# A 512-byte write per DMA engine ahead of the first store, and the last tile stored in two pieces instead of four

## The chip, the cores and the metric

One core of a Trainium2 chip. The metric is the device time in microseconds (us) of one execution; lower is better.

## The reference

The input `x` is 32 x 512 x 2048 numbers of float32. With `x1` the first 1024 columns and `x2` the last 1024:

```python
silu_x1 = x1 * (1 / (1 + np.exp(-x1)))
return (silu_x1 * x2).astype(np.float32)
```

134.22 MB are read and 67.11 MB written, each byte once. There is no matrix product.

## The kernel before

The 16,384 rows are cut into 16 tiles (0 to 15) of 1024 rows: 128 partitions with K = 8 consecutive rows each, so that one partition's share is contiguous in memory, 64 KB of input and 32 KB of output. Loads are issued by ScalarE and stores by SyncE, so they stand on two DMA rings. A ring is a queue of transfers; each DMA here is cut into packets that 16 DMA engines carry (a load is 128 packets of 64 KB in the records), and at its end every engine writes 4 bytes: 560 such records for the 35 DMAs of the kernel before. I read them as the report of completion, since the trace has 560 landings as well, each 0.3 to 0.7 us after its record when both are paired in order of time. SBUF is the memory on the chip that holds the tiles, HBM the large memory that holds `x` and the output. Two input buffers and two output buffers hold whole tiles.

```python
K = 8
KC = 2
in_pool  = ctx.enter_context(tc.tile_pool(name="in_pool", bufs=2))
out_pool = ctx.enter_context(tc.tile_pool(name="out_pool", bufs=2))
# ... cut: plan, view(), the first load moved ahead of the start barrier
load(0)                       # nc.scalar.dma_start: the ring of the loads, q10 in the profile
load(1)
for i in range(n_tiles):
    xt = loaded.pop(i)
    last = i == n_tiles - 1
    ov = view(out_flat, i)
    ot = out_pool.tile([P, K, half], dt, name="ot")
    for c in range(0, k, KC):                 # four steps of 2 rows
        ce = min(c + KC, k)
        nc.scalar.activation(out=ot[:, c:ce, :], in_=xt[:, c:ce, :half], func=...Silu)
        nc.vector.tensor_mul(out=ot[:, c:ce, :], in0=ot[:, c:ce, :], in1=xt[:, c:ce, half:])
        if last:                              # the last tile leaves in four pieces
            nc.sync.dma_start(out=ov[:, c:ce, :], in_=ot[:, c:ce, :])
    if not last:                              # nc.sync: the ring of the stores, q1 in the profile
        nc.sync.dma_start(out=ov, in_=ot[:, :k, :])
    if i + 2 < n_tiles:
        load(i + 2)                           # this input buffer is free again
```

The load of tile i + 2 waits for the multiplies of tile i. Each store waits for multiplies.

## Time and profile before

| | before |
|---|---|
| median of the 3 runs | 470.78 us (470.76 to 470.87) |
| span of the profiled run | 468.87 us |
| DMA rate over the span | 429 GB/s |
| VectorE, ScalarE busy | 30%, 25% |

These lines are of the page of the kernel before: its span; the busy time of the engines; the mean busy share of the 16 DMA engines in 40 slices, in tenths; the packets; the two rings with packets, MB and the share of 16 engines' time; the chain of waits by engine and by line; and the DMA issues with their size in KB and the median time from issue to landing.

```profile
span 468.9 us, 269 instructions
...
DVE 142.3 (30%) x64; ACT 118.2 (25%) x65; POOL 0.2 (0%) x4
...
DMA  9899999999999998999999999999999989999998
...
DMA packets 5042, 201.35 MB, mean 429 GB/s; under 512 B 560, under 2 KB 560, under 8 KB 560
...
q10 hardware_dynamic: 2304, 134.22, 66.4%
q1 hardware_dynamic: 2736, 67.11, 33.2%
...
DMA 80%; DVE 15%; ACT 3%; DVEq 0%; issue 0%
DMA xt<-in_x_dram 80%; DVE ot L92 15%; ACT ot L87 3%; DVEq L128 0%
...
out_dram<-ot SPq DMA_DIRECT2D x15, 4096.0 KB, 39.8
out_dram<-ot SPq DMA_DIRECT2D x4, 1024.0 KB, 5.7
xt<-in_x_dram ACTq DMA_DIRECT2D x16, 47.1
```

The DMA row is at 9 nearly everywhere, and the two rings' packets take 66.4% + 33.2% = 99.6% of the engines' time. The chain of waits says the same from the other end: 80% of the span is waiting for loads. VectorE and ScalarE are idle for 70% and 75% of the span, and stand in the chain for 18% of it, mostly between a load's landing and the issue of the load two tiles later.

The end of the run, from the timeline of the kernel before (start, duration, engine, line, operation, how often, and the idle time before it with what ended it):

```profile
...
start us, us, engine line op out<-in xcount [idle before <-releaser]
451.03 7.31 ACT L87 ACTIVATE ot<-xt 128x2048 f32<-128x2048 f32 x4 [21.57 <-DMA xt<-in_x_dram]
452.97 8.90 DVE L92 TENSOR_TENSOR ot<-ot,xt 128x2048 f32<-128x2048 f32 x4 [19.98 <-ACT ot L87]
455.29 6.94 SPq L98 DMA_DIRECT2D out_dram<-ot  x4
```

The last tile's Silu begins when its load has landed, at 451.03 us; its first store piece is issued 4.26 us later, after the first multiply.

**The packet records.** The trace also has a record for each DMA packet: ring, start, duration and size, but not the engine. I strung them to engines by joining each record to one that ended within some 5 ns of its start. In the kernel before, an engine's string is gapless from its first packet to its last, but for a fetch of instructions (0.3 us) on two engines: a packet of 64 KB (load) takes 2.418 us, one of 32 KB (store) 1.213, one of 8 KB 0.309, and a completion write of 4 bytes 0.009. Here is one engine around the first store (start us, duration us, ring, bytes):

```
 33.264  2.441  q10 65536
 35.701  3.180  q10 65536     <- 0.76 us too long, once
 38.878  1.213  q1  32768     <- first packet of the first store
 40.087  2.418  q10 65536
 42.501  1.213  q1  32768
 43.711  0.009  q10 4         <- completion of a load: a turn of its own
 43.717  1.213  q1  32768
 44.926  2.418  q10 65536
```

From the first store on, the rings take strict turns, one packet each: of the 3,887 pairs of neighbours strung this way between 34 and 428 us, 3,869 change the ring. A 4-byte completion write uses a whole turn, like the one of 0.009 us at 43.711 us, which stands alone between two store packets. From start to start of its load packets (65,536 bytes in 2.414 us) this case makes 16 x 27.15 = 434.4 GB/s, and none of the 2,048 load packets took less than the usual 2.418 us. That no packet can be faster is my estimate from these numbers; it was not shown. If it holds, the only time to win lies where packets do not follow each other at that pace: 1.1 us before the first packet, about 0.6 us in the first load packets, 0.87 us per engine (mean of 16) in the long packet ahead of the first store, and 1.2 us from the last packet to the end of the span.

### The profile page before, as it was taken

The numbers are of one execution on the slowest core, as the hardware profiler recorded it, in microseconds if no ns is written. First come the engines' busy times: TensorE is split into PE (matmuls) and PEld (weight loads), VectorE is DVE, ScalarE is ACT, GpSimd is POOL, SyncE is SP. The second block draws the span as 40 slices with busy tenths as digits, with TensorE's granted clock in tenths as the row PEclk, the third lists the DMA queues.
The fourth block names the chain that finished last, engine by engine and source line by source line (L and its number), as shares of the span: only waits on it lengthen the run. The fifth ranks groups of instructions, "written<-read, shape, count | busy, mean of one in ns | idle before, by whom it ended". The sixth has DMA issues, their size and how long they took to land.

```text
span 468.9 us, 269 instructions
## 1 busy us (share of the span) xinstructions
DVE 142.3 (30%) x64; ACT 118.2 (25%) x65; POOL 0.2 (0%) x4
## 2 busy tenths in 40 slices
DVE  0070705106061160601507025070250702407034
ACT  1142406023060330603206032060420604106051
POOL 0000000000000000000000000000000000000000
DMA  9899999999999998999999999999999989999998
GB/s 431 375 447 403 447 447 447 403 419 431 447 447 403 447 492 363 442 492 391 458 403 439 456 447 403 409 442 447 447 403 444 467 386 447 442 419 481 400 409 354
DMA packets 5042, 201.35 MB, mean 429 GB/s; under 512 B 560, under 2 KB 560, under 8 KB 560
## 3 DMA queue, kind: packets, MB, share of 16 engines
q10 hardware_dynamic: 2304, 134.22, 66.4%
q1 hardware_dynamic: 2736, 67.11, 33.2%
q14 instruction: 2, 0.02, 0.0%
HBM read 134.22 MB, written 67.11 MB: 429 GB/s over the span
## 4 chain that ended last, share of the span: by engine, by line
DMA 80%; DVE 15%; ACT 3%; DVEq 0%; issue 0%
DMA xt<-in_x_dram 80%; DVE ot L92 15%; ACT ot L87 3%; DVEq L128 0%
## 5 line engine op out<-in xcount | busy, mean ns | idle before, releaser
L92 DVE TENSOR_TENSOR ot<-ot,xt 128x2048 f32<-128x2048 f32 x64 | 142.3, 2286 | 319.5 <-ACT ot L87 319.5
L87 ACT ACTIVATE ot<-xt 128x2048 f32<-128x2048 f32 x64 | 116.9, 1897 | 338.8 <-DMA xt<-in_x_dram 338.8
L87 ACT ACT_TABLE_LOAD x1 | 1.3, 1283 | 1.3 <-PEq L117 1.3
L117 POOL MEMSET const-uint8-127<- 128x1 uint8 x1 | 0.1, 102 | 0.0
L117 POOL MEMSET const-bfloat16-1.0<- 128x1 bf16 x1 | 0.1, 101 | 0.0
L117 POOL MEMSET const-float32-0.0<- 128x1 f32 x1 | 0.1, 98 | 0.2 <-issue 0.2
L117 POOL MEMSET const-float32-1.0<- 128x1 f32 x1 | 0.1, 98 | 0.0
## 6 DMA issues: line engine op xcount, KB each, us to landing
out_dram<-ot SPq DMA_DIRECT2D x15, 4096.0 KB, 39.8
out_dram<-ot SPq DMA_DIRECT2D x4, 1024.0 KB, 5.7
xt<-in_x_dram ACTq DMA_DIRECT2D x16, 47.1
```

The source lines that it names most:

```text
L87: nc.scalar.activation(out=ot[:, c:ce, :], in_=xt[:, c:ce, :half], func=mybir.ActivationFunctionType.Silu,)
L92: nc.vector.tensor_mul(out=ot[:, c:ce, :], in0=ot[:, c:ce, :], in1=xt[:, c:ce, half:],)
L117: nc = _bacc.Bacc("TRN2", target_bir_lowering=False, num_devices=1)
```

## The change

The small write goes from the first tile's result to rows of the last tile that are overwritten later, 512 bytes for each of 16 partitions and so for each DMA engine. It is issued just ahead of the first store, on the same ring. The last tile is stored in two pieces of 4 rows, each as soon as its two multiplies are done, with 16 KB instead of 8 KB per packet. The intent that can be read from the code is to let something small meet the ring of the stores before the first large store does, and to spend fewer packets on the last tile.

```diff
     K = 8
     KC = 2
+    KS = 4
 ...
-            if last:
-                nc.sync.dma_start(out=ov[:, c:ce, :], in_=ot[:, c:ce, :])
+            if last and ce % KS == 0:
+                nc.sync.dma_start(out=ov[:, ce - KS:ce, :], in_=ot[:, ce - KS:ce, :])
+        if i == 0:
+            nc.sync.dma_start(
+                out=view(out_flat, n_tiles - 1)[:16, k - 1, :128], in_=ot[:16, k - 1, :128]
+            )
         if not last:
             nc.sync.dma_start(out=ov, in_=ot[:, :k, :])
```

## The prediction

> **What bounds it now.** The 16 DMA engines. The page shows 201.35 MB moved at 429 GB/s; VectorE is busy 30%, ScalarE 25%. The packet records of one engine, put in order, show no gap over some 5 ns from its first packet (1.1–1.8 us) to the last end (467.6 us of a 468.87 us span): load packets of 64 KB take 2.418 us, store packets of 32 KB 1.213, of 8 KB 0.309. Only two places lose time: the first load packets (about 0.6 us) and, once, the load packet just before each engine's first store packet, 3.2–3.4 us instead of 2.42 (about 0.87 us). The chain of waits (80% DMA) agrees: per tile 47 us from issue to landing, then Silu and multiplies.
>
> From the first store on, the two rings alternate strictly, one packet each; a 4-byte completion write uses a whole turn. [...]
>
> **What the change does.**
>
> 1. The small write adds two turns to the store ring (512 bytes and a 4-byte completion) before any bulk packet. During each the load ring still sends 64 KB, so from then on stores are two 32 KB turns behind. Cost: estimated 0.03 us of DMA time. Loads should land about 2.4 us (2 x 1.21) earlier: the last Silu group starts near 448.6 us instead of 451.03. No byte is saved; the final store backlog grows by as much.
>
> 2. It is issued at the same moment as the first store (both wait for the tile's last multiply, 32.7 us), so I expect it to pay the one-time 0.87 us instead of the store, not to remove it. 25% that it largely vanishes, 10% that it is paid twice.
>
> 3. Two 2 MB pieces replace four of 1 MB. Packets become 16 KB; from the slope between the three sizes I estimate 0.607 us each, so 16 cost 9.71 us where 32 of 8 KB cost 9.79; two completion turns go. Gain about 0.1 us. But the first piece waits for two multiplies. In the old schedule that would be 457.5 us, while the previous store's packets run dry at 457.0–457.4; with about 1 us from issue to first packet (read at the first load) the engines would idle 1 to 1.5 us. Step 1 pays for this: the multiplies start 2.4 us earlier, so the first piece is issued near 455.1 us and finds the ring busy. The second half alone should lose about 1 us.
>
> **On the critical path.** Only DMA occupancy counts: +0.03 −0.1, perhaps −0.87.
>
> **Prediction.** 470.6 us, range 469.8 to 471.2. Faster by over 2%: 0.5%; within 2%: 99%; slower: 0.5%.
>
> **What would show it.** Step 1: the last Silu group about 2.4 us earlier, two more load packets before the first 32 KB store packet. Step 2: the long load packet (3.2 us) still there, now before the 512-byte packet. Step 3: 256 packets of 16 KB near 0.61 us, the first piece issued at 455 ± 1 us, no gap before it, last end near 467.5 us.
>
> **What would make it wrong.** The 0.87 us belongs to the size of the first bulk packet, so a small one spares it (469.8); the store ring runs empty after the small write, so that it is paid twice; the completion write uses no turn of its own there (then 1.2 us of lead and a small gap before the last pieces, up to 471.3); or the last store waits for something new because it overwrites the rows of the small write.

## More of the kernel before

Silu of tile i waits for the load of tile i, and for the store of tile i - 2, which frees its output buffer.

What ScalarE waited for in the whole run, from the view of the waits of the kernel before (total, times, longest):

```profile
...
engine line waited for: us in total, times, longest us
ACT ot L87 <- DMA xt<-in_x_dram: 338.8, 16, 22.1
...
```

All 16 waits of Silu are for loads, none for an output buffer.

## The result, and the profile after

| | before | changed |
|---|---|---|
| median of 6 runs each | 470.89 us (470.76 to 471.38) | 470.88 us (470.57 to 471.02) |
| ratio, 95% interval | | 0.9998 (0.9985 to 1.0011) |
| span of the profiled run | 468.87 us | 469.2 us |

A ratio here and below is the mean time of one kernel's fast runs over that of the kernel before in the same rounds, so not quite the ratio of the medians. The time did not change. The run did. The page of the changed kernel, the lines that answer to those above:

```profile
span 469.2 us, 267 instructions
...
DVE 142.3 (30%) x64; ACT 118.2 (25%) x65; POOL 0.2 (0%) x4
...
DMA  9999999999999999999999999999999999999988
...
DMA packets 4787, 201.35 MB, mean 429 GB/s; under 512 B 545, under 2 KB 561, under 8 KB 561
...
q10 hardware_dynamic: 2304, 134.22, 66.4%
q1 hardware_dynamic: 2480, 67.12, 33.2%
...
DMA 79%; DVE 15%; ACT 3%; DVEq 0%; issue 0%
DMA xt<-in_x_dram 79%; DVE ot L93 15%; ACT ot L88 3%; DVEq L135 0%
...
out_dram<-ot SPq DMA_DIRECT2D x15, 4096.0 KB, 46.9
out_dram<-ot SPq DMA_DIRECT2D x2, 2048.0 KB, 8.1
xt<-in_x_dram ACTq DMA_DIRECT2D x16, 47.1
out_dram<-ot SPq DMA_DIRECT2D x1, 8.0 KB, 9.5
```

The engines work as before and the rate is the same 429 GB/s. There are fewer packets (q1: 2,480 for 2,736). But a store now takes 46.9 us from issue to landing, where it took 39.8, while loads still take 47.1. The end of the run in the timeline of the changed kernel:

```profile
...
start us, us, engine line op out<-in xcount [idle before <-releaser]
449.24 7.31 ACT L88 ACTIVATE ot<-xt 128x2048 f32<-128x2048 f32 x4 [21.69 <-DMA xt<-in_x_dram]
451.18 8.89 DVE L93 TENSOR_TENSOR ot<-ot,xt 128x2048 f32<-128x2048 f32 x4 [20.11 <-ACT ot L88]
455.70 4.73 SPq L99 DMA_DIRECT2D out_dram<-ot  x2
```

The last Silu group starts at 449.24 us, 1.79 us earlier than before, and the first of the two pieces is issued at 455.70 us, close to the 455.29 us of the kernel before, although it waits for two multiplies instead of one. ScalarE's waits in the changed kernel are still all for loads:

```profile
...
engine line waited for: us in total, times, longest us
ACT ot L88 <- DMA xt<-in_x_dram: 337.0, 16, 22.1
...
```

The packet records of one engine of the changed kernel around the first store:

```
 35.688  2.418  q10 65536
 38.102  0.027  q1  512       <- the small write
 38.126  3.476  q10 65536     <- the long packet, 1.06 us too long
 41.600  0.009  q1  4         <- completion of the small write
 41.606  0.009  q10 4         <- completion of load 1
 41.610  1.213  q1  32768     <- first packet of the first store
 42.820  2.418  q10 65536
```

The small write used two turns of the store ring. In the kernel before, two store packets of 1.21 us had gone out before load 1 completed; here none had. Load 1 is complete at 41.61 instead of 43.72 us on this engine, and the loads keep the lead to the end. The start of each tile's first Silu, us:

| tile | before | changed |
|---|---|---|
| 0 | 21.88 | 21.93 |
| 1 | 44.54 | 42.49 |
| 2 | 73.53 | 71.54 |
| 8 | 247.55 | 245.60 |
| 15 | 451.03 | 449.24 |

Nothing was saved: what the loads gained, the stores lost. After the last load, only stores are left, and there are more of them than before: 7.90 MB start after the end of the last load packet, where it was 7.34. The last packet ends at 467.99 us (slowest engine; 467.63 before), the median engine at 467.18 (467.02 before).

The lead has a price that the time does not show. The store of tile i - 2 must land before Silu of tile i may start, because it frees the output buffer. From the times of issue and landing in the two traces:

| | store of tile 6 landed | load of tile 8 landed | the store was ready ahead of Silu by |
|---|---|---|---|
| before | 240.21 us | 247.53 us | 7.34 us |
| changed | 245.34 us | 245.52 us | 0.26 us |

Over all tiles the reserve was 7.30 to 7.51 us before and is 0.19 to 0.28 us after. The shift adds up on both sides: in this table the load lands 2.0 us earlier and the store 5.1 us later. Silu starts 0.02 to 0.08 us after a load landed, so the changed kernel stands within 0.2 us of waiting for its own stores. In the packet records the completion write of such a store stands directly before that of the load, on nearly every engine and tile: the reserve is a single turn.

### The profile page after: what moved, and what is told of

Read it like the earlier page. It is cut to its first block, busy times and chain, and to the rows that moved or that the text cites. A ratio compares the mean times of both kernels' runs of the same rounds, so it can differ in the third digit from the quotient of the medians.

```text
span 469.2 us, 267 instructions
## 1 busy us (share of the span) xinstructions
DVE 142.3 (30%) x64; ACT 118.2 (25%) x65; POOL 0.2 (0%) x4
## 3 DMA queue, kind: packets, MB, share of 16 engines
q1 hardware_dynamic: 2480, 67.12, 33.2%
## 4 chain that ended last, share of the span: by engine, by line
DMA 79%; DVE 15%; ACT 3%; DVEq 0%; issue 0%
DMA xt<-in_x_dram 79%; DVE ot L93 15%; ACT ot L88 3%; DVEq L135 0%
## 6 DMA issues: line engine op xcount, KB each, us to landing
out_dram<-ot SPq DMA_DIRECT2D x15, 4096.0 KB, 46.9
xt<-in_x_dram ACTq DMA_DIRECT2D x16, 47.1
```

## The experiments

Two questions. What does the small write do: does it move the order of turns only (my theory), or does it save something at the first store that the two pieces give back (the rival)? And what is the long packet: the first use of a ring, or something of the first bulk store?

### Two pieces without the small write

```diff
 changed kernel
-        if i == 0:
-            nc.sync.dma_start(out=view(out_flat, n_tiles - 1)[:16, k - 1, :128], in_=ot[:16, k - 1, :128])
```

> The last tile in two pieces, without the small write. Turn theory (the small write only puts the loads two turns ahead, which the late first piece needs): last Silu group at 451.0 us as in the kernel before, first piece issued at 457.5 us, all 16 engines idle some 1 to 1.5 us from 457.0-457.4 us until its first packet, last end of a packet near 468.8 us, time 471.6 to 472.2 us, 0.8 to 1.3 us over the kernel before. Rival (the small write is of no use, the two pieces cost nothing by themselves): no gap, 470.8 us.

471.34 us (471.16 to 471.44, 5 runs) against 470.87; ratio 1.0010 (0.9997 to 1.0022). The timeline of this kernel, two pieces alone:

```profile
...
start us, us, engine line op out<-in xcount [idle before <-releaser]
451.22 7.31 ACT L88 ACTIVATE ot<-xt 128x2048 f32<-128x2048 f32 x4 [21.62 <-DMA xt<-in_x_dram]
453.16 8.90 DVE L93 TENSOR_TENSOR ot<-ot,xt 128x2048 f32<-128x2048 f32 x4 [20.03 <-ACT ot L88]
457.68 4.74 SPq L99 DMA_DIRECT2D out_dram<-ot  x2
```

The Silu group is back at 451.22 us and the first piece is issued at 457.68 us. Now the busy time in three stretches around that moment (bounds, length, busy time of VectorE, ScalarE and GpSimd, granted clock, DMA share, GB/s; this view counts a packet in full in the stretch in which it starts, so a share can read over 1 or too low), for the kernel before:

```profile
...
core 0: us, DVE busy (x) ACT busy (x) POOL busy (x), PEclk, DMA share, GB/s
445.00:457.00 12.00, 4.03 (x2) 5.97 (x4) 0.00 (x0) 1.00 1.00 431
457.00:459.00 2.00, 2.00 (x2) 1.34 (x1) 0.00 (x0) 1.00 0.95 401
459.00:468.00 9.00, 2.87 (x2) 0.00 (x0) 0.00 (x0) 1.00 0.89 377
...
```

for two pieces alone:

```profile
...
core 0: us, DVE busy (x) ACT busy (x) POOL busy (x), PEclk, DMA share, GB/s
445.00:457.00 12.00, 3.84 (x2) 5.78 (x4) 0.00 (x0) 1.00 1.01 437
457.00:459.00 2.00, 2.00 (x2) 1.53 (x1) 0.00 (x0) 1.00 0.31 131
459.00:468.00 9.00, 3.06 (x2) 0.00 (x0) 0.00 (x0) 1.00 1.03 437
...
```

and for the changed kernel:

```profile
...
core 0: us, DVE busy (x) ACT busy (x) POOL busy (x), PEclk, DMA share, GB/s
445.00:457.00 12.00, 5.82 (x3) 7.31 (x4) 0.00 (x0) 1.00 1.01 434
457.00:459.00 2.00, 2.00 (x2) 0.00 (x0) 0.00 (x0) 1.00 0.92 393
459.00:468.00 9.00, 1.07 (x1) 0.00 (x0) 0.00 (x0) 1.00 0.89 382
...
```

Between 457 and 459 us the view gives a DMA share of 31% with two pieces alone, against 95% before and 92% with the small write added. It counts packets by their start, so 31% is not the busy time itself; the packet records give that: each engine stands still once, for 0.50 to 1.40 us (mean 1.00, so half of the 2 us), between the last packet of the store before and the first packet of 16 KB near 458.5 us. That is 0.8 us after the issue, and about 0.5 us after the end of the 0.33 us that the issue itself takes. Before, and in the changed kernel, no engine has a gap there.

So the gap is shown, at the size expected. Its cost in time came out smaller than I expected: 0.47 us by the medians, where I had said 0.8 to 1.3, and the interval of the ratio just includes no change. Part of the reason is in the records: the engine that was last to finish the store before waited least (0.50 us). All engines start together again and end within 0.2 us of each other (468.35 to 468.53), where they ended within 0.8 us before (466.81 to 467.63). So the slowest engine ends 0.9 us later and the median one 1.4.

### The small write without the two pieces

```diff
 changed kernel
-    KS = 4
+    KS = 2
```

> The small write, with the last tile still in four pieces. Turn theory: last Silu group near 449.2 us as in the changed kernel (1.8 us earlier than before), first piece issued near 453.5 us, no gap, but the end does not move: last packet end 467.6 to 468.2 us, time 470.8 to 471.2 us, within 0.3 us of the kernel before. Rival (the small write saves the wait at the first store and the two pieces give it back): 470.0 us, about 0.8 us faster than the kernel before. In both, the long load packet of 3.3 to 3.5 us follows the 512-byte packet, as in the changed kernel.

471.08 us (471.03 to 471.32, 5 runs) against 470.87; ratio 1.0004 (0.9991 to 1.0018). The last Silu group starts at 449.34 us and no engine has a gap near 457 us. The long packet follows the 512-byte packet and costs 0.81 us per engine, so it was not saved, and the 0.8 us that the rival promised did not come. The small write alone gains nothing.

### The small write, early

```diff
 two pieces alone
+            if i == 0 and c == 0:      # after the first of four multiplies
+                nc.sync.dma_start(out=view(out_flat, n_tiles - 1)[:16, k - 1, :128], in_=ot[:16, 0, :128])
```

> The small write issued after the first of the four multiplies (about 26 us), some 7 us ahead of the first store, last tile in two pieces. First-use-of-ring theory: the long load packet (0.9 to 1.1 us over 2.42) comes with the small write, before 35 us, and none stands near the first 32 KB store packet. First-bulk-store theory: none before 35 us, and one of 3.2 to 3.5 us just before the first 32 KB store packet near 38 to 41 us. If each change from idle to busy of the ring costs, both. The turns of the small write are used up while only loads run, so the loads gain no lead: last Silu group at 450.5 to 451.2 us and a gap of about 1 us before the last tile's first piece.

One look: 471.86 us. This kernel contains both halves of the change; only the moment of the small write differs. Its two turns fall at 30.8 and 33.2 us, while only loads run, and no lead comes of them: the last Silu group starts at 451.57 us, the first piece is issued at 458.04 us, and the engines stand still for 0.50 to 1.85 us (mean 1.44) before it. No packet is long at the small write. The long one (1.07 us per engine) is still right before the first 32 KB store packet:

```
 30.789  0.027  q1  512       <- the small write, early
 30.812  2.418  q10 65536
 33.226  0.009  q1  4
 33.232  2.436  q10 65536
 35.665  3.465  q10 65536     <- the long packet
 39.126  1.213  q1  32768     <- first packet of the first store
```

So it is not the presence of the small write that closes the gap at the end but the turns it takes while store packets are waiting; and having used the ring before does not remove the long packet.

### Two small writes

```diff
 changed kernel
         if i == 0:
             nc.sync.dma_start(out=view(out_flat, n_tiles - 1)[:16, k - 1, :128], in_=ot[:16, k - 1, :128])
+            nc.sync.dma_start(out=view(out_flat, n_tiles - 1)[:16, k - 2, :128], in_=ot[:16, k - 2, :128])
```

> Two small writes one after the other ahead of the first store, last tile in two pieces. Turn theory: four turns instead of two, so the last Silu group starts another 1.2 to 2.4 us earlier than in the changed kernel (446.8 to 448.0 us), and the time stays at 470.9 us within 0.4, as nothing but the order moves. The one-time long load packet: if it belongs to the first use of the ring it stands right after the first 512-byte packet, as in the changed kernel; if it belongs to the first bulk store packet it stands right before the first 32 KB packet, two or more load packets later.

480.01 us (479.36 to 480.43, 4 runs) against 470.87; ratio 1.0193 (1.0179 to 1.0207). I had expected no change. The waits of this kernel say what I had left out:

```profile
...
engine line waited for: us in total, times, longest us
...
ACT ot L88 <- DMA out_dram<-ot: 313.9, 14, 25.1
ACT ot L88 <- DMA xt<-in_x_dram: 31.7, 2, 19.5
...
```

From tile 2 on, Silu waits for stores, not for loads. The store of tile 6 lands at 252.43 us, 3.60 us after the load of tile 8 (248.83), and holds the output buffer until then. The loads are early and nothing can use them. The 3.60 us are about one load packet and one store packet (2.414 + 1.209 from start to start). The records show where the time went. In the tiles from tile 2 on, some packets are too long, by up to 0.9 us; in sum packets lose 8.6 us per engine over the run, against 1.8 in the changed kernel. And the last tile is so late (Silu at 457.82 us, first piece issued at 464.29 us) that the engines stand still before its first piece for 1.1 us on the mean. 6.8 + 1.1 us are about the 7.8 us by which the median engine ends later (475.02 us for 467.18); the slowest ends at 476.80. Of the lengthening after 60 us, 99% lies in load packets, and nearly all of it where the rings alternate strictly, so it is not a ring that had run empty. Why packets lengthen in this state is open.

The long packet stands before the first 32 KB store packet again (it starts at 42.9 to 43.5 us), after both small writes, and not after the first of them.

### Two small writes and one small read

```diff
 two small writes
+        if i == 0:
+            tiny = tiny_pool.tile([16, 128], dt, name="tiny")
+            nc.scalar.dma_start(out=tiny[:, :], in_=view(x_flat, 0)[:16, 0, :128])
         if i + 2 < n_tiles:
             load(i + 2)
```

> The kernel with two small writes, which took 480.0 us, plus one small read of 512 bytes per engine on the ring of the loads, issued after the first tile ahead of the third load, its data unused. If the 9 us come from the order of turns (stores four turns behind, so that each store frees its output buffer some 3.6 us after the load of the tile that needs it): the small read gives two turns back to the stores, each store lands 0 to 3 us before the load of the tile two later, Silu waits for loads again, and the time is 470.6 to 471.6 us. If the 9 us come from the number or the placing of small writes in themselves: 479 to 481 us again.

470.95 us (470.75 to 471.68, 5 runs) against 470.95; ratio 1.0001 (0.9987 to 1.0015). The small read costs the load ring two turns, as each small write costs the store ring two, and the loss of 9 us is gone. ScalarE's waits in this kernel:

```profile
...
engine line waited for: us in total, times, longest us
ACT ot L89 <- DMA xt<-in_x_dram: 337.6, 16, 22.5
...
```

All are for loads again. Each store lands 0.2 us before the load of the tile two later, the same reserve as with one small write. The small read is the only difference between the two kernels, and its data are not used; so the 9 us belong to the balance of turns. The direct test of the wait, a third output buffer, was not run.

### Where the long packet comes from

Seven more kernels went to the long packet. Their times say little about it: with all but load1_on_store_ring, the last Silu group starts 1.9 to 5.7 us later than in the kernel before, and the engines stand still before the last tile's first piece for 0.4 to 1.5 us on the mean, as with two pieces alone. The table gives the edit against the kernel before, and what was lost per engine (packet durations over the usual ones, summed over the 16 engines and divided by 16), read from one profile of each kernel. hbm_copy_start has 6 runs. The kernel before took 471.05 us in the rounds of the first three (one run) and 471.03 in those of the other four (11 runs).

| kernel | edit, on the kernel before | lost, and where | time, us |
|---|---|---|---|
| store0_on_load_ring | `(nc.scalar if i == 0 else nc.sync).dma_start(out=ov, ...)` | 1.19 us in the load packet before the first store, on the load ring; 0.21 us where the store ring is first used (56 us) | 471.83 |
| load1_on_store_ring | `(nc.sync if i == 1 else nc.scalar).dma_start(out=xt, ...)` | 0.73 us in the first store packet and 0.75 us in the load packet after it | 481.75 |
| store6_on_load_ring | `(nc.scalar if i == 6 else nc.sync).dma_start(out=ov, ...)` | 0.97 us before the first store; 0.21 us where the store ring, run empty, starts again (230 us) | 472.56 |
| early_8k | 8 KB per engine written to HBM from `ot[:16, 0:2, :]` after the first multiply | 0.01 us at it and just after it; 1.17 us around the first 32 KB store packet, in the load packet before it (14 engines) or in those before and after it (2 engines) | 471.90 |
| early_32k | 32 KB per engine written to HBM from `xt[:16, 0:4, :]`, 22 us | 2.65 us in that packet itself, none at the first store | 475.14 |
| hbm_copy_start | 8 KB per engine from the input to the output in HBM, at the start | 0.91 us before the first 32 KB store packet | 471.88 (6 runs) |
| sbuf_copy_early | 8 KB per engine from SBUF to SBUF, first tile | 1.06 us around that copy, most of it in the load packets just after it; none at the first store | 471.72 |

**store0_on_load_ring**, expected:

> The kernel before, with the first store issued on the ring of the loads, which has been in use from the start; the store ring is first used by the second store, about 55 us. First-use-of-ring theory: no long packet at the first store, a load packet of 3.2 to 3.5 us just before the second store's first packet (55 to 70 us). First-bulk-store theory: a packet over its usual time by 0.8 to 1.1 us at the first store, none at the second.

With the first store on the ring that had been in use from the start, the long packet is there, and the later first use of the store ring costs only 0.21 us. So nearly all of it goes with the first bulk store and not with the ring.

**load1_on_store_ring**, expected:

> The kernel before, with the second load issued on the ring of the stores, so that this ring is first used by a load within the first 3 us. First-use-of-ring theory: no long load packet at the first store, any cost of first use falls in the first 6 us. First-bulk-store theory: still a load packet of 3.2 to 3.5 us just before the first 32 KB store packet, 35 to 45 us.

Having carried a load does not spare the store ring the cost: a load packet of 2.99 to 3.49 us stands right after the first store packet, in place of before it. This run is not as clean as I wanted: both first loads shared the engines, the first Silu group began at 39.22 us instead of 21.88, and all engines were idle for 10 us before the first store, so that the first store packet was slow too. That idleness makes up nearly all of the 10.7 us by which it was slower.

**store6_on_load_ring**, expected:

> The kernel before, with the store of the seventh tile issued on the ring of the loads, so that the store ring runs empty in the middle of the run (about 215 to 240 us) and is used again by the eighth. One-time theory (first use of the ring, or first bulk store): only the long load packet at 36 to 39 us, no other above 2.9 us. Idle-to-busy theory: a second one of 3.2 to 3.5 us where the store ring starts again.

The ring that had run empty cost 0.21 us where it started again, not 0.9. Neither of my two expectations held exactly: the second cost exists, but it is a quarter of the first.

**early_8k**, expected:

> The kernel before, with a write of 8 KB per DMA engine (16 partitions, rows overwritten later) on the store ring, issued after the first multiply at about 26 us, while only loads run. So far the long load packet (0.9 to 1.1 us too long) always stands right before the first 32 KB store packet. If the first sizable store packet of any size draws the whole cost: a load packet about 0.9 us too long just before the 8 KB packet (28 to 34 us), none before the first 32 KB one. If the cost grows with the packet: about 0.2 us at the 8 KB packet and 0.6 us or more at the first 32 KB one. If only the steady alternation of loads and stores draws it: nothing at the 8 KB packet, 0.9 us at the first 32 KB one.

An 8 KB store did not draw the cost; the first 32 KB packet does, in full.

**early_32k**, expected:

> The same with 32 KB per engine, sent from the first input tile at about 22 us. If a first bulk packet of 32 KB pays once and for all: a load packet 0.9 us too long before it, 24 to 30 us, and none before the first store near 39 us. If only the steady alternation draws it: the other way round.

Once a 32 KB packet has been sent, the first store has no long packet. The 2.65 us are three times the usual cost, and why is open. All 16 engines send from the same 16 partitions here, unlike a store of 128 partitions, but that alone does not explain it: the packets of early_8k came from 16 partitions too and took the usual 0.309 us.

**hbm_copy_start**, expected:

> The kernel before, with a copy of 8 KB per engine from the input straight to output rows that are overwritten later, issued on the store ring at the very start, beside the first load, where the engines' first packets are slow anyway. If the one-time cost is that of the first write of each engine to HBM, whatever its source: no long load packet at the first store, about 0.3 us more DMA time for the copy, time 0.3 to 0.6 us under the kernel before (470.3 to 470.6 us). If it needs SBUF as the source or a sizable packet: the long load packet of 3.2 to 3.5 us stays before the first 32 KB packet, and the time is 0.2 to 0.5 us over the kernel before.

471.88 us (471.07 to 472.70, 6 runs) against 471.03; ratio 1.0013 (1.0001 to 1.0025). The long packet stayed, so it is not the first write to HBM. This was my candidate for a faster version; if anything it was slower, by 0.1% with an interval that barely excludes no change. Its trace shows part of why: the last Silu group starts at 452.89 us, 1.86 us later than in the kernel before, and 14 of the 16 engines stand still before the first piece of the last tile, for 0.38 us on the mean of 16.

**sbuf_copy_early**, expected:

> The kernel before, with a copy of 8 KB per engine from SBUF to SBUF on the store ring, issued early in the first tile (the output is wrong on purpose in those rows if the copied row has not been used). If the one-time cost is that of the first read from SBUF by each engine: a load packet too long just before the copy and none before the first 32 KB store packet. If it is that of writing to HBM: nothing at the copy, 0.9 us before the first 32 KB store packet.

The copy inside SBUF drew the whole cost, in the 8 KB packets and the load packets after them, and the first store then had none. The sum, 1.06 us against 0.87, shows that the cost was moved, not removed. The output was right; the copied row had been used by then.

What follows: the one-time loss of about 0.9 us is not that of the first use of a ring, nor of the first write to HBM. It comes with the first 32 KB store packet (early_8k: 1.17 us), or with a copy from SBUF to SBUF of 8 KB (1.06 us), and not with a store of 512 bytes (the load packet after it took the usual 2.418 us in the early small write) or of 8 KB (0.01 us). The cases with 8 KB rest on one profile each. What it is inside the engine these runs do not say, and I leave it open. For this change one thing is enough: a small write ahead of it neither removes nor shrinks it.

## Why the prediction was right

It said 470.6 us, in the range 469.8 to 471.2; measured were 470.88. The sign of so small a difference was never to be seen: the runs of the kernel before alone spread from 470.76 to 471.38.

- **The bound** was right: the engines stay full, at 429 GB/s before and after.
- **Step 1, two turns.** Right in kind. The loads gained 2.05 us at tile 1 and 1.79 us at tile 15; I had said 2.4 and 448.6 us for the last Silu group, and it was 449.24. Two turns of 1.21 us went as said, at a cost of 0.027 + 0.009 us where I had estimated 0.03; the long packet, longer by 0.16 us on the mean in this run, took some of it back. My sign of it, "two more load packets before the first 32 KB store packet", was off: it was one load packet and one completion write, which also fills a turn.
- **Step 2, the long packet is not removed.** Right in outcome: 0.87 us per engine before, 1.03 after, and 0.81 with the small write alone. Wrong in place: I expected it ahead of the 512-byte packet, and it came after that packet, ahead of the first 32 KB one. What I named as the way to be wrong, that it belongs to the size of the first bulk packet, is half true: it does go with the bulk packet, and for that very reason a small one does not spare it.
- **Step 3, two pieces.** The 16 KB packets take 0.611 us, 0.607 from start to start, as estimated. The gap without step 1 is shown (mean 1.00 us per engine, near 458 us), and step 1 closes it: first piece at 455.70 us, no gap. The cost of the second half alone was mis-sized: I said about 1 us, the medians give 0.47 and the profiled spans 469.7 against 468.87.
- **What the prediction left out** is the output buffer. It said that the stores fall two turns behind and did not ask who waits for stores. The reserve fell from 7.3 us to 0.2 us. The prediction survived this by 0.2 us, which was luck: nothing in it said that the reserve would suffice; my expectation for two small writes, built on the same omission, missed by 9 us.

## What to carry to other kernels

In this kernel, which keeps the DMA engines full, a small DMA on one of two rings cost almost no bandwidth (0.04 us per engine) but two turns of order, and the shift lasted to the last tile; the store ring never ran empty in between. Here the order was worth something only where somebody waited: it paid for a later first piece at the end (455.70 us, no gap), and it took nearly all the reserve of the output buffers (7.3 us before, 0.2 us after). So before shifting the order, read for each buffer how long before its next use it comes free, and see whether the shift fits into that.
